# A two-layer trunk on one core: layer 0's adaLN scale in seven blocks of 128 to 512 features in place of five

## The chip, the cores and the metric

The kernel runs on one core of one Trainium2 chip. Its measure is the device time of one execution in microseconds. Three runs of the kernel before gave a median of 1295.17 us, from 1294.84 to 1297.33.

The engines' names in the rows are PE (TensorE, matrix products), PEld (its weight loads), DVE (VectorE), ACT (ScalarE), POOL (GpSimd) and SP (SyncE, which issues most of the loads).

## The reference

A trunk of two layers runs over 128 context tokens and 256 latent tokens, 2048 features each. Before each mixer there is an adaLN step, and layer 0's is where the change lies:

```
m = silu(cond) @ w_mod + b_mod          # (2048 -> 6144), once for c_ctx, once for c
shift, scale, gate = split(m, 3)
h = rms_norm(x, g) * (1 + scale) + shift
proj = h @ w_in                         # q, k, v, conv and gate parts
...
x = x + gate * (concat([a, b]) @ w_out)
```

All is float32. The context tokens take the modulation of c_ctx, the latent tokens that of c. Products of tokens with weights must hold float32 accuracy.

## The kernel before

**Tokens and products.** The state is kept transposed, features on partitions: `xT` is 128 partitions x 16 chunks (k = 0 to 15, 128 features each) x 384 tokens. A product in float32 is made from three matmuls of half-length operands: both operands are split into a high and a low part (`hhi`, `hlo` of the tokens, `whi`, `wlo` of the weights) and hi x hi, hi x lo and lo x hi are added in PSUM. `whi` is a ScalarE cast (L283), `wlo` a VectorE subtraction (L284).

**The scale.** The adaLN vector is a product of two conditioning vectors with a 2048 x 2048 slice of the modulation weights: 16 MiB that are read once, in 16 tiles of 1 MiB. `gemv_block` (L122 to 145) makes one block of `nf` features: one *unit* per tile, with `2048 // nf` matmuls each, that hold a 32-column window of the conditioning vectors `cst` as weights and stream the tile's `nf` columns. Four accumulators stand in the four 32-partition groups of one PSUM tile (`gv`). A finished block is *handed over*: ScalarE copies it (`gs`, L143), PE transposes it in pieces of 128 (L172), VectorE adds the four groups (L158) and the bias (L160), and for the scale forms (1 + s) * g (L163). The PSUM pool of `gv` has one buffer. Tiles land in a ring of four SBUF slots (L592).

**The front of the program.** The loop at L607 to 627 goes over the scale's blocks. For each, with priority, it issues the block's units, the load of the block's part of `xT`, and `make_h`, which forms `hhi` (ScalarE, L289) and `hlo` (VectorE, L290) from `xT` and the scale; then, per chunk k, `q_unit` (L594) loads 512 KB of q weights, splits them and issues 18 matmuls of 512 columns, and `square` gathers the squares for the norm. The norm's own factor (`rs0`, `rb0`) is applied later, so the q products need the scale alone. After it the stage that the text calls wkv makes the k and v products (`tok_unit`, L347, matmuls at L355) on the shifted tokens. Four blocks of 512 features of layer 0's shift are made there in the same manner, one ahead of every four chunks (`shifted`, L643); `hhi` and `hlo` come from L302 and L303.

**What sets the order.** Every engine has one queue of instructions. The order in each is decided by a scheduler that runs the program through a simulated timeline when the kernel is built; a priority (`first()`), a chain that keeps all loads of SP in program order (L95 to 101), and a few added dependences steer it. So where units of a gemv stand between the products is the scheduler's choice, and it can change far behind an edit.

Of the kernel before, what the change touches and what calls it, by code (L numbers as in the profile page):

```python
# [20 lines left out]
D = 2048  # L21
# [22 lines left out]
SCALE_AT = (11,)  # L44
RA = 1.2
RB = 1.1
GRID_W = 64
GROUPS = ((0, 0, SEQ), (1, SEQ, T))

# [2 lines left out]
def trunk(ctx: ExitStack, tc: tile.TileContext, d: dict, o: dict):  # L52
# [25 lines left out]
    def vcol(name, i):  # L78
        return vec(name)[:, i:i + 1]
# [5 lines left out]
    cst = const.tile([P, 2 * KC + 30], F32, name="cst")  # L85
# [61 lines left out]
    def mod_tile(layer, part):  # L147
        m = const.tile([P, KC, 2], F32, name=f"mod{layer}{part}")
        mods[layer, part] = m
        return m  # L150
# [14 lines left out]
    def mod_part(layer, part, widths=(512, 512, 512, 512), f0=0):  # L165
        if (layer, part) not in mods:
            mod_tile(layer, part)

        def consume(f0, nf, gs, pc):
            n = nf // P  # L170
            for i in range(n):
                nc.tensor.transpose(pc[:, i * P:(i + 1) * P], gs[:, i * P:(i + 1) * P], ident)  # L172
            sl = slice(f0 // P, (f0 + nf) // P)
            mod_finish(layer, part, sl, pc[:, :nf].rearrange("p (k g r) -> p k r g", g=4, r=32)[:, :, 0:2, :])
        units = []
        for nf in widths:
            units += gemv_block(d[f"mod_w{layer}"][4 * part + f0 // 512], f0 % 512, nf, lambda k: cst[:, 2 * k:2 * k + 32],
                                lambda gs, ps, f0=f0, nf=nf: consume(f0, nf, gs, ps))
            f0 += nf
        return units  # L180
# [419 lines left out]
                    nc.tensor.matmul(pq[b][t], lhsT=x[:, k, tt], rhs=y[:, 0, 512 * b:512 * b + 512],  # L600
                                     start=(k == 0 and n == 0), stop=(k == KC - 1 and n == 2))

    widths = (256, 256, 512, 512, 512)
    scale_q = mod_part(0, 1, widths)
    pq = [[acc("q0") for t in range(NT)], [acc("q1"), acc("q1"), aux("q1")]]
    av, square = square_sum(nc.gpsimd)
# [151 lines left out]
    def ln_out(c):  # L758
        ln["out"] = nc.vector.tensor_tensor(apad[:, c, :T], apad[:, c, :T], ln["r"], ALU.mult).ins
        nc.scalar.activation(apad[:, c, :T], apad[:, c, :T], AF.Silu, scale=vcol("ln_g0", c), bias=vcol("ln_b0", c))  # L760
    bg["rate"] = RB

# [190 lines left out]
def _by_rows(a):  # L953
    return a.reshape(a.shape[0], -1, P).transpose(2, 1, 0)


def _blocks(w, width):
    return w.reshape(KC, P, -1, width).transpose(2, 1, 0, 3)


def _layout(inputs):
    a = {name: np.asarray(x) for name, x in inputs.items()}
    out = {name: a[name] for name in _AS_IS}
    out["vecs"] = np.concatenate([a[name].reshape(n, P).T for name, n in _VECS], axis=1)
    for name in ("c_ctx", "c"):
        out[f"row_{name}"] = a[name].reshape(-1)
    for l in range(2):
        out[f"modT{l}"] = a[f"mod_w{l}"].T.reshape(48, P, D)
    out["xT"] = _by_rows(np.concatenate([a["x_prompt"][0], a["x_sample"][0]]))
    out["cw"] = _by_rows(np.concatenate([a["conv_w0"], a["short_w1"]]))  # L970
    for l in range(2):
        out[f"cache_k{l}"] = a[f"cache_k{l}"][0].transpose(2, 1, 0)
        out[f"mod_w{l}"] = _blocks(a[f"mod_w{l}"], 512)
        out[f"w_out{l}"] = _blocks(a[f"w_out{l}"], 256)
    w = a["w_in0"]
    out["wf0"] = _blocks(np.concatenate([w[:, :3 * CW], w[:, 3 * CW + 1536:]], axis=1), 256)
    out["wq0"] = _blocks(w[:, 3 * CW:3 * CW + 1024], 1024)
    out["wkv0"] = _blocks(w[:, 3 * CW + 1024:3 * CW + 1536], 512)
    out["wt1"] = _blocks(a["w_in1"][:, :1536], 512)
    out["wf1"] = _blocks(a["w_in1"][:, 1536:], 256)  # L980
    return out


def _tables():
# [3 lines left out]
    tok = np.arange(DEC)  # L988
    ar = (tok // GRID_W).astype(f)[:, None] * inv
    ac = (tok % GRID_W).astype(f)[:, None] * inv  # L990
    ang = np.concatenate([ar, ar, ac, ac], axis=-1).astype(f)
# [26 lines left out]
```

## Time and profile before

| | |
|---|---|
| median of three runs | 1295.17 us (1294.84 to 1297.33) |
| the profiled execution | 1295.11 us |
| its span | 1293.3 us, so 1.81 us lie outside it |
| PE busy | 1260.2 us, 97% of the span |
| VectorE, ScalarE, GpSimd busy | 873.3, 540.3 and 91.7 us |
| DMA | 258.00 MB, mean 199 GB/s |

The span runs from the first to the last recorded instruction of the core. The chain of waits is followed back from the last instruction, at each step to what released it, so its shares say where the end was decided. In a timeline row the first number is the start and the second the length; adjacent matmuls overlap in their recorded lengths, and the distance from start to start is what one costs in a row. A row's `x16` says that it stands for 16 records; a float32 matmul of a gemv unit leaves two, so the 8 matmuls of a 256-wide unit stand as x16 and the 4 of a 512-wide one as x8.

### The profile page before, as it was taken

How to read it: one execution, taken by the hardware profiler on the slowest of the kernel's cores; microseconds unless marked ns; L12 is line 12 of the kernel's file. 1: busy time of each engine (PE TensorE's matmuls, PEld its weight loads, DVE VectorE, ACT ScalarE, POOL GpSimd, SP SyncE). 2: the span in 40 equal slices, each digit the busy share in tenths (PEclk: the TensorE clock that was granted, in tenths of full speed). 3: DMA queues.
4: the chain of work that ended last, by engine and by line, in shares of the span. 5: the costliest groups of instructions: out<-in, count | busy, mean ns of one | idle time of the engine just before them, and what ended most of it. 6: DMA issues, size and time to landing. Idle time of an engine off the chain costs nothing.

```text
span 1293.3 us, 17857 instructions
## 1 busy us (share of the span) xinstructions
PE 1260.2 (97%) x6892; PEld 1114.7 (86%) x6892; DVE 873.3 (68%) x1507; ACT 540.3 (42%) x936; POOL 91.7 (7%) x129
## 2 busy tenths in 40 slices
PE   6999999999999999999999999999999999999996
PEld 4566676778888889999999988899999999999996
DVE  2244688989899867999776933354544599994443
ACT  3345422564455555533363623354444432343331
POOL 0211100000000000111000000000000011101110
PEclk9999999999999999999999999999999999999998
DMA  9989987878665444677543444433333578744322
GB/s 363 402 311 350 346 315 293 324 247 290 225 200 172 169 150 147 187 259 249 163 129 115 131 124 124 138 114 115 99 98 98 171 267 275 261 148 127 119 66 98
DMA packets 70503, 258.00 MB, mean 199 GB/s; under 512 B 7377, under 2 KB 11729, under 8 KB 65425
## 3 DMA queue, kind: packets, MB, share of 16 engines
q1 hardware_dynamic: 58768, 207.71, 47.4%
q0 software_dynamic: 11504, 49.04, 10.8%
q8 instruction: 54, 0.88, 0.3%
q14 instruction: 33, 0.26, 0.1%
q10 hardware_dynamic: 144, 0.10, 0.0%
HBM read 253.15 MB, written 3.67 MB: 199 GB/s over the span
## 4 chain that ended last, share of the span: by engine, by line
PE 95%; issue 2%; DMA 1%; ACT 1%; DVE 1%; POOL 0%; POOLq 0%; SPq 0%; DVEq 0%; ACTq 0%
PE pf L376 67%; PE pt L355 10%; PE q L600 6%; PE gv L139 5%; PE s_ps L499 2%; PE o_ps L524 2%; PE pT_ps L520 1%; DMA ring<-in_mod_w 1%; PE gv L172 1%; PE qT_ps L485 0%; PE gv L664 0%; ACT mix L452 0%; DMA raw<-in_mod_w 0%; DVE y L929 0%; ACT whi L283 0%
## 5 line engine op out<-in xcount | busy, mean ns | idle before, releaser
L376 PE MATMUL pf<-hhi,whi 128*128 128x384 f32 (+1 forms) x1664 | 570.0, 343 | 2.1 <-ACT whi L283 2.1
L376 PE MATMUL pf<-hlo,whi 128*128 128x384 f32 (+1 forms) x1664 | 569.2, 342 | 0.0
L376 PE MATMUL pf<-hhi,wlo 128*128 128x384 f32 (+1 forms) x1664 | 564.5, 343 | 1.2 <-DVE wlo L284 1.2
L284 DVE TENSOR_TENSOR wlo<-raw,whi 128x1024 fp32r<-128x1024 f32 x256 | 312.9, 1223 | 299.3 <-ACT whi L283 294.4
L283 ACT CAST whi<-raw 128x1024 fp32r<-128x1024 f32 x256 | 268.3, 1049 | 485.0 <-PE pf L376 276.5
L376 PEld LDWEIGHTS pf<-hhi,whi 128*128 128x128 f32 x1664 | 313.5, 188 | 24.0 <-issue 14.0
L376 PEld LDWEIGHTS pf<-hhi,wlo 128*128 128x128 f32 x1664 | 313.4, 189 | 15.9 <-issue 7.3
L376 PEld LDWEIGHTS pf<-hlo,whi 128*128 128x128 f32 x1664 | 314.0, 189 | 5.0 <-issue 2.7
L690 DVE SCALAR_TENSOR_TENSOR cv<-apad,cw,cv 128x399 f32<-128x399 f32 x240 | 138.3, 627 | 0.1
L207 DVE CUSTOM_DVE_ANT_0 area<-area,crow 128x1024 f32<-128x1024 f32 x112 | 132.5, 1218 | 4.5 <-PE o_ps L524 4.5
L355 PE MATMUL pt<-wlo,hhi 128*128 128x512 f32 x192 | 75.8, 395 | 0.0
L355 PE MATMUL pt<-whi,hhi 128*128 128x512 f32 x192 | 75.5, 396 | 0.0
L355 PE MATMUL pt<-whi,hlo 128*128 128x512 f32 x192 | 74.2, 396 | 0.0
L91 POOL DMA_DIRECT2D area<-in_modT x56 | 29.6, 529 | 552.0 <-DVE sm L207 206.0
L276 POOL TENSOR_TENSOR sacc<-sacc,sqf 128x384 f32<-128x384 f32 x28 | 33.4, 1194 | 176.3 <-ACT sqf L275 175.5
L600 PE MATMUL q<-whi,hhi 128*128 128x512 f32 x96 | 41.2, 429 | 4.4 <-ACT hhi L289 4.4
L355 PEld LDWEIGHTS pt<-whi,hhi 128*128 128x128 f32 x192 | 36.0, 188 | 10.9 <-ACT hhi L302 1.7
L355 PEld LDWEIGHTS pt<-whi,hlo 128*128 128x128 f32 x192 | 35.9, 188 | 9.9 <-DVE wlo L284 1.7
L355 PEld LDWEIGHTS pt<-wlo,hhi 128*128 128x128 f32 x192 | 36.1, 188 | 9.1 <-issue 0.8
L139 PE MATMUL gv<-ring,cst 128*32 128x512 f32 (+1 forms) x288 | 35.6, 582 | 8.4 <-DMA ring<-in_mod_w 7.5
L507 ACT ACTIVATE pr<-s_ps,nm 128x384 f32<-128x384 f32 (+1 forms) x48 | 24.4, 508 | 45.8 <-DVE nm L506 34.6
L600 PE MATMUL q<-wlo,hhi 128*128 128x512 f32 x96 | 40.6, 423 | 0.0
(181 smaller groups left out, 986.4 us busy)
## 6 DMA issues: line engine op xcount, KB each, us to landing
raw<-in_wf SPq DMA_DIRECT2D x144, 512.0 KB, 4.1
ring<-in_mod_w SPq DMA_DIRECT2D x32, 1024.0 KB, 7.5
raw<-in_w_out SPq DMA_DIRECT2D x64, 512.0 KB, 4.1
area<-in_modT POOLq DMA_DIRECT2D x56, 512.0 KB, 5.3
raw<-in_mod_w SPq DMA_DIRECT2D x48, 512.0 KB, 5.2
raw<-in_wq SPq DMA_DIRECT2D x32, 512.0 KB, 8.9
raw<-in_wt SPq DMA_DIRECT2D x24, 512.0 KB, 3.5
lent<-in_modT POOLq DMA_DIRECT2D x8, 1024.0 KB, 8.2
```

The costliest lines, as they stand in the source:

```text
L91: ins = nc.gpsimd.dma_start(dst, src).ins
L139: nc.tensor.matmul(ps[32 * g:32 * g + 32, :nf], lhsT=stat(k), rhs=raw[:, i % raw.shape[1], :], start=(k < 4), stop=(k >= KC - 4))
L207: ins = nc.vector.tensor_tensor_reduce(out=raw if g else junk, in0=raw, in1=crow[:, g, h * n:(h + 1) * n], scale=1.0, scalar=0.0, op0=ALU. ...
L276: eng.tensor_tensor(av, av, s, ALU.add)
L283: nc.scalar.copy(dst_hi, src)
L284: order["split"] = nc.vector.tensor_tensor(dst_lo, src, dst_hi.bitcast(F32), ALU.subtract).ins
L355: nc.tensor.matmul(pp[t], lhsT=x[:, k, tt], rhs=y[:, i, :], start=(k == 0 and n == 0), stop=(k == KC - 1 and n == 2))
L376: ins = nc.tensor.matmul(pp[j][:, :n], lhsT=x[:, i, fj], rhs=y[:, k, :n], start=(begin and k % 8 == 0 and m == 0), stop=(end and k % 8 == ...
L499: nc.tensor.matmul(ps, lhsT=mix[:, h0 + h, t * P:(t + 1) * P], rhs=kT[:, kv, c0:c0 + nk * P], start=True, stop=True)
L524: nc.tensor.matmul(po, lhsT=v[:, slots[j], kv * HD:(kv + 1) * HD], rhs=pT[:, j, :], start=(j == 0), stop=(j == nk - 1))
L600: nc.tensor.matmul(pq[b][t], lhsT=x[:, k, tt], rhs=y[:, 0, 512 * b:512 * b + 512], start=(k == 0 and n == 0), stop=(k == KC - 1 and n == 2))
L690: nc.vector.scalar_tensor_tensor(st["o"], apad[:, c, j:j + CVW], cw[:, c, j:j + 1], st["o"], ALU.mult, ALU.add)
```

## The change

The list `widths` has seven blocks in place of five. For blocks under 512 wide the weights come from new arrays, `scale128` (features 0 to 255) and `scale256` (features 256 to 1023), which hold the same numbers laid out block by block: per block 128 partitions, then 16 chunks, then the block's features in a row. A tile for the ring is then one piece of 8 KB per partition; before, a 256-wide block was cut from a 512-wide one, in eight pieces of 1 KB per partition. The blocks of 512 are read as before. The same bytes are read, and 128-wide blocks have one unit of 16 matmuls of 128 columns each. Lines after the insertions stand 1 (from L44) to 5 (from L179 on) further down in the changed kernel: L139 is L140 there, L172 is L173, L158 is L159, L160 is L161, L284 is L289, L303 is L308, L355 is L360, L600 is L605.

```
--- before.py
+++ after.py
@@ -44,6 +44,7 @@
 SCALE_AT = (11,)
 RA = 1.2
 RB = 1.1
+NARROW = {128: (0, 256), 256: (256, 1024)}
 GRID_W = 64
 GROUPS = ((0, 0, SEQ), (1, SEQ, T))
 
@@ -174,7 +175,11 @@
             mod_finish(layer, part, sl, pc[:, :nf].rearrange("p (k g r) -> p k r g", g=4, r=32)[:, :, 0:2, :])
         units = []
         for nf in widths:
-            units += gemv_block(d[f"mod_w{layer}"][4 * part + f0 // 512], f0 % 512, nf, lambda k: cst[:, 2 * k:2 * k + 32],
+            if nf < 512:
+                w, at = d[f"scale{nf}"][(f0 - NARROW[nf][0]) // nf], 0
+            else:
+                w, at = d[f"mod_w{layer}"][4 * part + f0 // 512], f0 % 512
+            units += gemv_block(w, at, nf, lambda k: cst[:, 2 * k:2 * k + 32],
                                 lambda gs, ps, f0=f0, nf=nf: consume(f0, nf, gs, ps))
             f0 += nf
         return units
@@ -600,7 +605,7 @@
                     nc.tensor.matmul(pq[b][t], lhsT=x[:, k, tt], rhs=y[:, 0, 512 * b:512 * b + 512],
                                      start=(k == 0 and n == 0), stop=(k == KC - 1 and n == 2))
 
-    widths = (256, 256, 512, 512, 512)
+    widths = (128, 128, 256, 256, 256, 512, 512)
     scale_q = mod_part(0, 1, widths)
     pq = [[acc("q0") for t in range(NT)], [acc("q1"), acc("q1"), aux("q1")]]
     av, square = square_sum(nc.gpsimd)
@@ -972,6 +977,8 @@
         out[f"cache_k{l}"] = a[f"cache_k{l}"][0].transpose(2, 1, 0)
         out[f"mod_w{l}"] = _blocks(a[f"mod_w{l}"], 512)
         out[f"w_out{l}"] = _blocks(a[f"w_out{l}"], 256)
+    for nf, (f0, f1) in NARROW.items():
+        out[f"scale{nf}"] = _blocks(a["mod_w0"][:, D + f0:D + f1], nf)
     w = a["w_in0"]
     out["wf0"] = _blocks(np.concatenate([w[:, :3 * CW], w[:, 3 * CW + 1536:]], axis=1), 256)
     out["wq0"] = _blocks(w[:, 3 * CW:3 * CW + 1024], 1024)
```

The scheduler's order differs on all engines at many small places in the first third of the program. PE's queue at the start of the kernel before (`gv` is a block's accumulator, `ring` the loaded tiles, `q0` and `q1` the q accumulators):

```order
L139 MATMUL gv_108<-ring_98,cst_87 32x256 x16
L172 MATMUL gv_108<-ident_79,gs_127 128x128 x2
L600 MATMUL q0_101<-whi_145,hhi_93 128x512
L600 MATMUL q0_101<-wlo_146,hhi_93 128x512
L600 MATMUL q0_102<-whi_145,hhi_93 128x512
```

and of the changed kernel:

```order
L140 MATMUL gv_108<-ring_98,cst_87 32x128 x16
L173 MATMUL gv_108<-ident_79,gs_126 128x128
L140 MATMUL gv_162<-ring_98,cst_87 32x128 x16
L605 MATMUL q0_101<-whi_139,hhi_93 128x512
L605 MATMUL q0_101<-wlo_140,hhi_93 128x512
```

The order groups like rows: before, the first `x16` holds the units of both tiles, 8 matmuls each. Now the first block is a single tile of 16 narrower matmuls and one transpose, and the second block's unit stands ahead of the first q product.

PE's queue in the wkv stage of the kernel before, where the second block of the shift is handed over (`pt0` to `pt2` are the k and v accumulators of the three token groups):

```order
L355 MATMUL pt2_790<-whi_979,hlo_94 128x512
L139 MATMUL gv_1001<-ring2_99,cst_87 32x512 x4
L139 MATMUL gv_1001<-ring_98,cst_87 32x512 x4
L172 MATMUL gv_1001<-ident_79,gs_1022 128x128 x4
L139 MATMUL gv_1106<-ring_98,cst_87 32x512 x4
L355 MATMUL pt0_788<-whi_1060,hhi_93 128x512
```

and of the changed kernel:

```order
L360 MATMUL pt2_836<-whi_1025,hlo_94 128x512
L140 MATMUL gv_1047<-ring2_99,cst_87 32x512 x4
L140 MATMUL gv_1047<-ring_98,cst_87 32x512 x4
L173 MATMUL gv_1047<-ident_79,gs_1068 128x128 x4
L360 MATMUL pt0_834<-whi_1106,hhi_93 128x512
L360 MATMUL pt0_834<-wlo_1107,hhi_93 128x512
```

The first unit of the next shift block (`gv_1106`) stood between the transposes and the first product; now the product follows the transposes, and that unit (`gv_1152`) comes nine products later.

VectorE's queue at the same handover, before:

```order
L284 TENSOR_TENSOR wlo_1061<-raw_1058,whi_1060 128x1024
L284 TENSOR_TENSOR wlo_1085<-raw_1082,whi_1084 128x1024
L158 TENSOR_REDUCE mod00_787<-gv_1001 128x8
L160 TENSOR_TENSOR mod00_787<-mod00_787,vecs_81 128x8
L303 SCALAR_TENSOR_TENSOR hlo_94<-h32_1030,mod00_787,hhi_93 128x128
```

and of the changed kernel:

```order
L159 TENSOR_REDUCE mod00_833<-gv_1047 128x8
L161 TENSOR_TENSOR mod00_833<-mod00_833,vecs_81 128x8
L289 TENSOR_TENSOR wlo_1107<-raw_1104,whi_1106 128x1024
L289 TENSOR_TENSOR wlo_1131<-raw_1128,whi_1130 128x1024
L308 SCALAR_TENSOR_TENSOR hlo_94<-h32_1076,mod00_833,hhi_93 128x128
```

The two weight splits stood ahead of the reduction of the finished block and stand behind it now. Further on, around 211 us of the profile before, VectorE's queue had one of its 128x2048 modulation sums (`lent`) ahead of the split `wlo_1651`:

```order
L717 TENSOR_TENSOR apad_1235<-pf1_1421,sgb_1418 128x256
L207 ISA lent_1239,sm101_1254<-lent_1239,crow_91 128x2048
L207 ISA sm101_1254 128x1
L284 TENSOR_TENSOR wlo_1651<-raw_1648,whi_1650 128x1024
L284 TENSOR_TENSOR wlo_1681<-raw_1678,whi_1680 128x1024
```

and the changed kernel has:

```order
L722 TENSOR_TENSOR apad_1281<-pf0_1466,sgb_1462 128x256
L289 TENSOR_TENSOR wlo_1697<-raw_1694,whi_1696 128x1024
L722 TENSOR_TENSOR apad_1281<-pf1_1467,sgb_1464 128x128
L722 TENSOR_TENSOR apad_1281<-pf1_1467,sgb_1464 128x256
L289 TENSOR_TENSOR wlo_1727<-raw_1724,whi_1726 128x1024
L212 ISA lent_1285,sm101_1300<-lent_1285,crow_91 128x2048
```

Both splits now stand ahead of that sum, the first of them between the products' evacuations (`apad`).

## Rows read from the trace of the kernel before

**Rows 1.** The page: span, busy time by engine (share, instructions), chain by line.
```profile
span 1293.3 us, 17857 instructions
...
PE 1260.2 (97%) x6892; PEld 1114.7 (86%) x6892; DVE 873.3 (68%) x1507; ACT 540.3 (42%) x936; POOL 91.7 (7%) x129
...
PE pf L376 67%; PE pt L355 10%; PE q L600 6%; PE gv L139 5%; PE s_ps L499 2%; PE o_ps L524 2%; PE pT_ps L520 1%; DMA ring<-in_mod_w 1%; PE gv L172 1%; PE qT_ps L485 0%; PE gv L664 0%; ACT mix L452 0%; DMA raw<-in_mod_w 0%; DVE y L929 0%; ACT whi L283 0%
```

**Rows 2.** Chain of waits, first 30 us; columns start us, length us, what.
```profile
1.66 7.70 DMA ring<-in_mod_w
...
21.31 1.00 PE gv L139 x16
22.31 0.43 PE q L600
22.74 0.55 PE gv L139 x4
...
23.72 0.99 PE gv L139 x12
24.71 3.90 PE q L600 x16
28.61 0.23 PE gv L172 x2
```

**Rows 3.** Timeline of the start; idle before and its releaser in brackets.
```profile
6.52 1.94 PE L139 MATMUL gv<-ring,cst 128*32 128x256 f32 x16 [6.52 <-DMA ring<-in_mod_w]
6.92 0.22 PEld L139 LDWEIGHTS gv<-ring,cst 128*32 128x32 f32 x4 [0.20 <-issue]
...
9.40 1.93 PE L139 MATMUL gv<-ring,cst 128*32 128x256 f32 x16 [0.95 <-DMA ring<-in_mod_w]
...
12.96 1.04 ACT L283 CAST whi<-raw 128x1024 fp32r<-128x1024 f32 x1 [0.23 <-DMA raw<-in_wq]
...
14.71 0.80 PE L600 MATMUL q<-whi,hhi 128*128 128x512 f32 x1 [2.19 <-ACT hhi L289]
...
18.29 0.63 PE L600 MATMUL q<-whi,hhi 128*128 128x512 f32 x1
...
18.71 0.63 PE L600 MATMUL q<-wlo,hhi 128*128 128x512 f32 x1
...
21.24 1.07 PE L139 MATMUL gv<-ring,cst 128*32 128x256 f32 x16
...
29.10 1.07 PE L139 MATMUL gv<-ring,cst 128*32 128x512 f32 x8 [0.27 <-DVE mod L158]
```

**Rows 4.** Windows; busy us and (x instructions), PE clock, DMA share, GB/s.
```profile
14.70:19.50 4.80, 4.79 (x11) 3.84 (x12) 1.97 (x5) 1.05 (x3) 0.00 (x0) 1.00 1.09 364
...
42.00:54.00 12.00, 9.04 (x40) 6.16 (x36) 5.55 (x14) 6.64 (x13) 0.00 (x0) 0.86 1.01 415
140.00:155.00 15.00, 13.76 (x77) 7.76 (x72) 8.26 (x20) 5.57 (x12) 1.95 (x3) 1.00 0.98 381
```

**Rows 5.** Timeline of PE, first product after the long handover.
```profile
45.72 0.50 PE L600 MATMUL q<-whi,hhi 128*128 128x512 f32 x1 [2.20 <-ACT hhi L289]
```

**Rows 6.** Timeline of two handovers in the wkv stage.
```profile
127.76 1.07 PE L139 MATMUL gv<-ring,cst 128*32 128x512 f32 x8 [0.28 <-DVE mod L158]
127.94 2.19 ACT L302 ACTIVATE hhi<-h,mod 128x128 fp32r<-128x128 f32 x6 [2.00 <-DVE mod L160]
...
128.76 0.51 PE L355 MATMUL pt<-whi,hhi 128*128 128x512 f32 x1
...
142.20 1.07 PE L139 MATMUL gv<-ring,cst 128*32 128x512 f32 x8 [0.35 <-DVE mod L158]
```

**Rows 7.** Timeline around 211 to 215 us, VectorE and the product behind it.
```profile
211.41 2.28 DVE L207 CUSTOM_DVE_ANT_0 lent<-lent,crow 128x2048 f32<-128x2048 f32 x1
...
213.61 2.35 DVE L284 TENSOR_TENSOR wlo<-raw,whi 128x1024 fp32r<-128x1024 f32 x2
...
214.89 0.44 PE L376 MATMUL pf<-hhi,wlo 128*128 128x384 f32 x1 [1.19 <-DVE wlo L284]
```

More of the change, by code (lines that the diff above doesn't have):

```diff
@@ L46 @@
 RB = 1.1
+NARROW = {128: (0, 256), 256: (256, 1024)}
 GRID_W = 64
@@ L176, in mod_part @@
         for nf in widths:
-            units += gemv_block(d[f"mod_w{layer}"][4 * part + f0 // 512], f0 % 512, nf, lambda k: cst[:, 2 * k:2 * k + 32],
+            if nf < 512:
+                w, at = d[f"scale{nf}"][(f0 - NARROW[nf][0]) // nf], 0
+            else:
+                w, at = d[f"mod_w{layer}"][4 * part + f0 // 512], f0 % 512
+            units += gemv_block(w, at, nf, lambda k: cst[:, 2 * k:2 * k + 32],
                                 lambda gs, ps, f0=f0, nf=nf: consume(f0, nf, gs, ps))
@@ L601, in q_unit @@
                                      start=(k == 0 and n == 0), stop=(k == KC - 1 and n == 2))
-    widths = (256, 256, 512, 512, 512)
+    widths = (128, 128, 256, 256, 256, 512, 512)
     scale_q = mod_part(0, 1, widths)
@@ L974, in _layout @@
         out[f"w_out{l}"] = _blocks(a[f"w_out{l}"], 256)
+    for nf, (f0, f1) in NARROW.items():
+        out[f"scale{nf}"] = _blocks(a["mod_w0"][:, D + f0:D + f1], nf)
     w = a["w_in0"]
```

## The prediction, made before the changed kernel was timed

> **What bounds the kernel now.** I read the page's busy shares first, then the chain of waits, then the windows and the timeline of the places that the change touches. TensorE (PE) is busy 1260.2 of 1293.3 us and holds most of the chain that ended last; DMA has 1% of it [rows 1]. So a microsecond counts only where PE stands idle, runs at the lower clock, or gets more to do. PE idles 33 us in all, and the front of the kernel has a good part of it. The chain of the first 30 us is DMA until 9.36, then come the second 1 MiB scale tile's matmuls, transposes, a VectorE/ScalarE handover, and the first q product at 14.71, which waited 2.19 us behind the transposes [rows 2, 3]. So the first scale block, not the q weights, sets when the products start. The weight loads do not set it: k=1's raw tile had landed by 12.96 [rows 3]. Later the chain is almost all PE, with a handover (copy, transposes, reduce, add, hhi) wherever a finished block gates the next products.
>
> The clock shows as spacing. At 18.29 and 18.71 two q products start 0.42 us apart, and a chain piece at 24.71 has 16 in 3.90 [rows 2, 3], 0.24 each: the levels 1.2 and 2.4 GHz. The window 14.70 to 19.50 prints 1.00 in its clock column although the products in it are 0.42 apart, so there I go by spacing; 42 to 54 prints 0.86, and it is the window of PE's 2.20 us wait before 45.72 [rows 4, 5]: (1 - 0.86) x 12 = 1.7 us lost at the lower level.
>
> **The change part by part.** The bytes stay the same: 16 tiles of 1 MiB for the scale. What changes is the blocks' size (128, 128, 256, 256, 256, 512, 512 features), the DMA pieces (8 KB in a row per partition, where 256-wide blocks took eight of 1 KB), and with these the scheduler's order up to about a third of the kernel.
>
> *Start.* Before, two tiles must land and two units of 8 matmuls run before the first block is whole. Now one tile gives block 0, features 0 to 127, enough for k=0. The loads now stand as tile, xT, raw, tile, xT, raw. How fast do they land? The first tile's unit starts at 6.52, the second's at 9.40 [rows 3], each as its tile lands: 1024 KB in 2.88 us, 356 KB/us. From 9.40 to the cast of k=1's raw tile at 12.96 come 384 KB of xT and two raw tiles, 1408 KB in 3.56 us, 395 KB/us. At 395 each tile saves 2.88 - 1024/395 = 0.29 us. Tile 1 then lands near 6.2. Its unit, transpose, reduce, add and hhi for k=0 need less than the five microseconds to 11.4, and k=0's raw tile lands near 8, so none of these is late. What is late is PE itself: in its new order the second block's unit stands ahead of the first q product. Its tile has 704 KB more before it than before (one xT part of 192 and one raw of 512): 704/395 = 1.78, so 9.40 + 1.78 - 2 x 0.29 = 10.60, say 10.65. Bounds: 10.2, if the overlap of transfers hides some of the 704, and 11.2, if short pieces never cost anything. A 128-wide unit is 16 matmuls of 128 columns, and no row shows one. The profile has two records for each float32 matmul, so a 256-wide unit (8 of 256 columns) stands as x16, 1.94 at the lower clock, and a narrow one would stand as x32. If each record cost what it does at 256 columns, it would be 3.9, the upper bound. The lower is 1.07, a unit at the higher clock. At that clock 16 records of 256 columns (21.24) and 8 of 512 (29.10) both take 1.07 [rows 3], so the columns set it, and they are the same in a narrow unit: I take 1.94. First q product: 10.65 + 1.94 + about 0.1 = 12.7 in place of 14.71, **-2.0 us**. From above +0.5 (tile at 11.2 and unit of 3.9: 15.2). From below -2.9 with the unit at the higher clock. Since PE now goes from the unit straight into the products, without the pause of 2.19, its clock may also rise sooner: five products at 0.24 in place of 0.42 would be 0.9 more, -3.8 in all. I count none of it, since no row shows when the clock rises after such a start.
>
> *Skill against row.* The window 42 to 54 moves 415 GB/s for 12 us [rows 4]. "DMA: Bandwidth & Descriptors" of the Trainium skill, section Specifications, gives about 358 GB/s as the HBM limit of one core. By that limit the 356 KB/us of the first two tiles would already be the ceiling, contiguous pieces would win nothing, the second tile would land at 11.2 and the sum would be 0.55 higher. The trace disagrees, since 415 is held.
>
> *Skill against row.* Weight loads at 6.92 lie inside the matmul stretch that runs from 6.52 to 8.46 [rows 3]. "TensorE: Matmul & The Clock Gate" of the Trainium skill, section The mechanism, says loads overlap matmuls in flight only where the row groups differ. Here all 128 rows are always in use, so by that rule a narrow unit, with twice the loads, would go toward 3.9 and the first product toward 14.7. The trace disagrees with the strict form.
>
> *Handovers in the q stage.* Two more 256-wide handovers come before the long ones. One costs, beside the unit itself, the transposes' 0.23 and the 0.27 that PE waits for the reduce [rows 2, 3]: 0.45 to 0.64 with the switches, so +1.1 for two. The transposes of one four-transpose handover go (4 x 0.115, -0.45), and a unit that ran in two cut pieces now runs whole: before, 0.43 and 0.55, 0.43 once more, and 0.99 [rows 2] for two products and the unit's 16 records, which in one piece are 2 x 0.24 + 1.00 = 1.48; -0.9, of which I take -0.8 for the switch that stays. Net **-0.1**. The long wait (2.20 before 45.72, and the 1.7 us lost at the lower level) does not vanish: the same sort of handover now stands before k=8, at about 60 us. Its cover is the same, so 0. DMA is not late there: a 512-wide block brings 6.75 MiB (scale 4, raw 2, xT 0.75), 17.1 us at the 415 GB/s of [rows 4], and PE needs 72 x 0.24 and 4 x 1.0, 21.3.
>
> *The wkv stage.* Here the new order is worse for PE. Before, right after the transposes PE ran the next block's first unit from 127.76, while ScalarE made hhi from 127.94; products went on at 128.76 [rows 6]. Now the products stand right behind the transposes, and the unit comes nine products later. The products can start near 127.94 + 0.36 + 0.05 = 128.35, 0.41 sooner, but the unit is paid later by itself: 1.2 (its 1.07, and 0.51 where a product in a row shows about 0.4 [rows 6]). So +0.8 each at two handovers, this one and the next (142.20, [rows 6]): +1.6. The unit comes in more pieces (+0.5). On VectorE the reduce and add now stand ahead of both wlo subtractions, 1.2 each as the pair of 2.35 [rows 7], which before were done by then; so the second product waits for wlo, +0.5, and hlo behind it, +0.3, and the copy gs +0.1. Sum **+3.0**; bounds +0.5 (the scheduler's view, all hidden but one unit's share) and +5 (both handovers also uncover the second wlo).
>
> *VectorE at 211.* PE waits 1.19 us at 214.89 for wlo, which stood behind a 2.28 us reduction on VectorE [rows 7]. In the new order that wlo stands ahead of the reduction, between the apad products. The idle goes: **-1.2**, bounds 0 (the raw tile or the cast is next) and -1.5.
>
> Everything else: VectorE +6 and ScalarE +4 small instructions, hidden beside PE; the order moves in many small places to about 560 us, with no sign that I can read: 0, bounds +-1.5.
>
> **Sum.** -2.0 - 0.1 + 3.0 - 1.2 = -0.3. The profiled execution took 1295.11 us, 1293.3 of them span. 1295.11 - 0.3 = **1294.8 us**; the median of the runs shown is 1295.17, 0.06 above the profiled one.
>
> **Rivals.** What a measurement of this kernel tells from no change is 0.2%, 2.6 us.
>
> 1. Faster: the long handover before k=8 comes while PE has products in hand, so its clock does not fall (-1.7), and the wkv handovers cost 1.2 in place of 3.0 (-1.8): 1291.3. For it: in the old order the block of features 1024 to 1535, the same one, was handed over before k=8 with products in hand. Against: the same unhidden chain of copy, transposes, reduce and hhi stands there in the new order.
> 2. Slower: the uncovered wkv handovers (no unit between transposes and products) bring the clock down, as after the wait at 45.72. Price 1.7 each, twice: 1294.8 + 3.4 = 1298.2. It decides from the point where PE's idle there resembles that of 42 to 45.7; before, the window 140 to 155 held 1.00 with shorter waits [rows 4], so it needs about a microsecond or more of extra idle.
> 3. The change doesn't do what it says: tile 2 at 11.2 and a unit at 3.9 us put the first product at 15.2, or shorter pieces bring nothing. Then the start gives +0.5 in place of -2.0: 1297.3, still within 0.2%.
>
> **How the numbers follow.** Forecast 0.40, rival 3 0.12, rival 1 0.28, rival 2 0.20. The forecast and rival 3 lie within 0.2% of 1295.17 (1292.6 to 1297.8); rival 1 is faster, and rival 2 slower: faster 0.28, same 0.52, slower 0.20. Range 1291.0 to 1298.8: from a little under rival 1 to a little over rival 2; the forecast alone, by its own terms' bounds, has 1292.5 to 1297.5.
>
> **What would show it.** The first q product at 12.7 and the second gv unit from 10.65 for 1.94; its neighbours' spacing falling to 0.24 sooner than at 19. In the wkv stage gv units standing behind products, idle of 0.8 or so before the first product of each block, and a wait for wlo. At 211, no wait of 1.2 for wlo. The prediction is wrong in its middle if the wkv windows differ from before by under 1 us or over 5, or if a clock dip appears or goes.

## The result, and the profile after

The changed kernel took **1303.74 us** (median of 6 runs, 1300.11 to 1307.91), the kernel before 1295.26 beside it (6 runs). The ratio is 1.0061, 95% interval 1.004 to 1.0083: slower by about 8.5 us, and outside the range of the prediction, which had 1294.8 and a range of 1291.0 to 1298.8. Its runs spread over 7.8 us, those of the kernel before over 2.5. The profiled execution is the slowest of the six, 1307.91 us, so its differences are shown by stage and then weighed with runs of other kernels.

The page of the changed kernel, against [rows 1]: PE is busy 8.3 us longer in a span 12.8 us longer, and VectorE and DMA hold 2% each of the chain, where they had 1% each.

```profile
span 1306.1 us, 17993 instructions
...
PE 1268.5 (97%) x6956; PEld 1121.8 (86%) x6956; DVE 875.0 (67%) x1513; ACT 543.4 (42%) x940; POOL 91.0 (7%) x129
...
PE 93%; DVE 2%; DMA 2%; ACT 1%; issue 1%; SPq 0%; DVEq 0%; ACTq 0%
```

The same line of the kernel before:

```profile
PE 95%; issue 2%; DMA 1%; ACT 1%; DVE 1%; POOL 0%; POOLq 0%; SPq 0%; DVEq 0%; ACTq 0%
```

The start, against [rows 3] (timeline; idle before and its releaser in brackets). The first product comes at 13.53 in place of 14.71, and the products are 0.24 apart from 17.53 on (three in 0.87; in the kernel before from 19.52 on). The copy `gs` of the first block stood behind a cast on ScalarE that waited for a raw tile (9.05), PE's transpose waited 2.00 us for it, and the handover ended at 11.62 (L161). The second unit starts at 11.66. Its tile came at the same moment: the load was issued at 2.60 and landed 8.9 us later, at 11.52, and the unit starts 0.14 behind that, as the first one starts 0.13 behind its tile (6.24 and 6.37). So either alone would have put the unit there, and the late copy by itself cost next to nothing.

```profile
6.37 1.94 PE L140 MATMUL gv<-ring,cst 128*32 128x128 f32 x32 [6.37 <-DMA ring<-in_scale]
...
9.05 1.04 ACT L288 CAST whi<-raw 128x1024 fp32r<-128x1024 f32 x1 [1.04 <-DMA raw<-in_wq]
10.00 0.26 ACT L144 COPY gs<-gv 128x128 f32<-128x128 f32 x1
...
10.31 0.48 PE L173 MATMUL gv<-ident,gs 128*128 128x128 f32 x1 [2.00 <-ACT gs L144]
...
11.46 0.16 DVE L161 TENSOR_TENSOR mod<-mod,vecs 128x2 f32<-128x2 f32 x1
...
11.66 1.94 PE L140 MATMUL gv<-ring,cst 128*32 128x128 f32 x32 [0.87 <-DVE mod L161]
...
13.53 0.80 PE L605 MATMUL q<-whi,hhi 128*128 128x512 f32 x1
...
17.53 0.87 PE L605 MATMUL q<-whi,hlo 128*128 128x512 f32 x3
18.24 0.39 PE L605 MATMUL q<-whi,hhi 128*128 128x512 f32 x1
18.47 0.39 PE L605 MATMUL q<-wlo,hhi 128*128 128x512 f32 x1
...
66.76 0.79 PE L605 MATMUL q<-whi,hhi 128*128 128x512 f32 x1 [2.62 <-ACT hhi L294]
```

The last of these rows ends the long wait of the q stage, now before k=8. The load of the second tile, in the list of loads issued between 2.5 and 2.7 us (KB, us to landing):

```profile
ring<-in_scale SPq DMA_DIRECT2D x1, 1024.0 KB, 8.9
```

The wkv stage, against [rows 6]. No unit stands between the transposes and the first product; PE waits 0.99 us for `hhi` at one handover and 1.54 at the next, and `wlo` and `hlo` come behind the reduce. No product waits for that `wlo`: the second one follows the first by 0.34 us (129.23), as in the kernel before (128.76 and 129.10).

```profile
128.32 1.22 DVE L289 TENSOR_TENSOR wlo<-raw,whi 128x1024 fp32r<-128x1024 f32 x1
128.44 2.19 ACT L307 ACTIVATE hhi<-h,mod 128x128 fp32r<-128x128 f32 x6 [0.30 <-DVE mod L161]
128.89 0.50 PE L360 MATMUL pt<-whi,hhi 128*128 128x512 f32 x1 [0.99 <-ACT hhi L307]
129.23 0.39 PE L360 MATMUL pt<-wlo,hhi 128*128 128x512 f32 x1
...
129.46 1.40 DVE L308 SCALAR_TENSOR_TENSOR hlo<-h,mod,hhi 128x128 fp32r<-128x128 f32 x4
...
144.77 0.50 PE L360 MATMUL pt<-whi,hhi 128*128 128x512 f32 x1 [1.54 <-ACT hhi L307]
```

Behind it, against [rows 7]. A gemv unit for the q bias waits 2.08 us for its raw tile, which the kernel before did not. A product waits 1.60 us for a `wlo` behind another 2.29 us sum on VectorE than in [rows 7]; the wait of 1.19 that [rows 7] has is gone. At 250.49 there is a wait of 3.10. The kernel before has two in that place, 1.36 and 1.45, so little was added there (and new_blocks_old_order below has 2.96).

```profile
193.88 1.05 PE L140 MATMUL gv<-raw,mix 128*32 128x512 f32 x4 [2.08 <-DMA raw<-in_wq]
...
206.05 1.12 PE L669 MATMUL gv<-gs,mix 128*128 128x512 f32 x2 [0.69 <-ACT gs L144]
...
207.81 2.29 DVE L212 CUSTOM_DVE_ANT_0 lent<-lent,crow 128x2048 f32<-128x2048 f32 x1
...
210.10 1.22 DVE L289 TENSOR_TENSOR wlo<-raw,whi 128x1024 fp32r<-128x1024 f32 x1
...
211.37 0.44 PE L381 MATMUL pf<-hhi,wlo 128*128 128x384 f32 x1 [1.60 <-DVE wlo L289]
...
250.49 0.69 PE L381 MATMUL pf<-hhi,whi 128*128 128x384 f32 x1 [3.10 <-ACT whi L288]
```

The two of the kernel before:

```profile
238.65 1.05 PE L139 MATMUL gv<-raw,cst 128*32 128x512 f32 x4 [1.36 <-DMA raw<-in_mod_w]
...
241.16 0.57 PE L376 MATMUL pf<-hhi,whi 128*128 128x384 f32 x1 [1.45 <-ACT whi L283]
```

The chain of waits tells how the raw tile came to be late. Its load was issued at 182.04, behind three other loads that SP issued from 180.15 on, and took 11.79 us. In the kernel before the same tile's load was issued at 178.58, took 6.8 us and had landed 7 us ahead of its unit (192.50). The chain of the changed kernel, then the load in the kernel before:

```profile
182.04 11.79 DMA raw<-in_wq
193.83 0.04 issue
193.88 1.05 PE gv L140 x4
```

```profile
raw<-in_wq SPq DMA_DIRECT2D x1, 512.0 KB, 6.8
```

Windows of the changed kernel (PE clock is the third last column), to [rows 4]. The clock column is below 1.00 in four of them: (1 - 0.83) x 20 = 3.4 us lost, 1.8, 3.4 and 1.8. It stays at 1.00 in 140 to 155, behind the waits of the wkv stage. The kernel before lost 1.7 in 42 to 54 and 1.8 in 240 to 260. Below, a *clock stretch* is a piece of the clock record at 1.2 GHz that costs 1.7 us, half of its length; a piece of twice the length counts as two.

```profile
60.00:80.00 20.00, 16.62 (x71) 10.44 (x72) 6.57 (x14) 8.07 (x16) 3.54 (x3) 0.83 0.87 345
140.00:155.00 15.00, 12.70 (x69) 7.10 (x69) 9.69 (x22) 7.35 (x13) 1.06 (x2) 1.00 0.99 368
180.00:200.00 20.00, 17.92 (x93) 14.54 (x93) 14.68 (x15) 4.23 (x5) 1.60 (x3) 0.91 0.96 359
240.00:260.00 20.00, 16.90 (x77) 11.93 (x76) 19.60 (x38) 13.24 (x50) 0.00 (x0) 0.83 0.97 370
280.00:300.00 20.00, 18.02 (x99) 12.08 (x98) 18.47 (x31) 11.85 (x27) 1.61 (x3) 0.91 0.69 224
```

and of the kernel before:

```profile
240.00:260.00 20.00, 18.84 (x93) 15.66 (x94) 19.29 (x38) 7.66 (x16) 0.00 (x0) 0.91 0.76 263
```

**PE's loss by stage.** Both kernels give PE the same work in another order. So I counted for every matmul record about the spacing that it has in a row at 2.4 GHz (0.2305 us for 512 columns of a product and 0.1745 for 384, where the trace's medians are 0.232 and 0.175, and 1.0 for a gemv unit of 1 MiB; the small error is the same in every kernel), and took the sum of what had been started from the time. The growth of that difference is what PE lost, whatever the order. Of it I took half of the time at 1.2 GHz as the clock's part, at the start by the products' spacing, behind it by the clock record. The stages are cut at the same amounts of work (10, 88, 156, 192, 600 us); "start" counts from the first tile's landing.

| us lost, net of the clock / by the clock | start | q | wkv | to 192 | 192 to 600 |
|---|---|---|---|---|---|
| kernel before | 3.05 / 6.46 | 6.98 / 1.71 | 6.73 / 0 | 7.80 / 0 | 32.59 / 1.71 |
| changed kernel | 1.89 / 5.57 | 7.44 / 3.41 | 10.17 / 0 | 11.96 / 1.71 | 33.31 / 5.12 |
| new_blocks_old_order | 2.06 / 4.52 | 8.24 / 1.71 | 6.70 / 0 | 7.83 / 0 | 32.55 / 1.71 |
| old_blocks_new_order | 3.04 / 6.57 | 6.99 / 1.71 | 10.15 / 0 | 12.10 / 3.41 | 32.86 / 0 |
| new_order_in_wkv_only | 1.55 / 4.62 | 8.28 / 1.71 | 9.81 / 0 | 7.83 / 0 | 32.67 / 0 |
| new_order_behind_wkv_only | 1.35 / 4.94 | 7.38 / 3.41 | 5.76 / 0 | 11.45 / 0 | 31.91 / 3.41 |
| old_wkv_in_new_places | 1.75 / 4.66 | 8.24 / 1.71 | 7.01 / 0 | 11.73 / 1.71 | 31.90 / 5.12 |
| blocks_of_256_early_norm | 1.56 / 4.75 | 4.43 / 0 | 9.69 / 0 | 7.80 / 0 | 33.29 / 1.71 |

The net losses repeat to a few tenths where the order is the same; the clock's part does not. In the q stage the two trade: where there are two clock stretches, the first begins while PE still waits (at 65.32 in the changed kernel, whose product starts at 66.76), and the net loss is some 0.8 lower.

### The profile page after: what moved, and what is told of

It reads as the page before. It is cut to its first block, busy times and chain, and to the rows that moved or that the text cites. A ratio compares the mean times of both kernels' runs of the same rounds, so it can differ in the third digit from the quotient of the medians.

```text
span 1306.1 us, 17993 instructions
## 1 busy us (share of the span) xinstructions
PE 1268.5 (97%) x6956; PEld 1121.8 (86%) x6956; DVE 875.0 (67%) x1513; ACT 543.4 (42%) x940; POOL 91.0 (7%) x129
## 4 chain that ended last, share of the span: by engine, by line
PE 93%; DVE 2%; DMA 2%; ACT 1%; issue 1%; SPq 0%; DVEq 0%; ACTq 0%
PE pf L381 65%; PE pt L360 10%; PE q L605 6%; PE gv L140 5%; PE s_ps L504 2%; PE o_ps L529 2%; DMA raw<-in_wq 1%; PE pT_ps L525 1%; DVE cv L695 1%; DMA raw<-in_wf 1%; ACT whi L288 1%; PE y_ps L907 1%; DVE wlo L289 0%; PE qT_ps L490 0%; PE gv L173 0%
## 5 line engine op out<-in xcount | busy, mean ns | idle before, releaser
L289 DVE TENSOR_TENSOR wlo<-raw,whi 128x1024 fp32r<-128x1024 f32 x256 | 313.9, 1227 | 288.7 <-ACT whi L288 283.8
L360 PE MATMUL pt<-whi,hhi 128*128 128x512 f32 x192 | 75.6, 397 | 2.5 <-ACT hhi L307 2.5
L360 PE MATMUL pt<-wlo,hhi 128*128 128x512 f32 x192 | 75.7, 394 | 0.0
L360 PE MATMUL pt<-whi,hlo 128*128 128x512 f32 x192 | 75.2, 398 | 0.0
L360 PEld LDWEIGHTS pt<-whi,hhi 128*128 128x128 f32 x192 | 36.0, 188 | 13.8 <-ACT hhi L307 3.8
L360 PEld LDWEIGHTS pt<-whi,hlo 128*128 128x128 f32 x192 | 35.9, 188 | 12.8 <-DVE hlo L308 2.0
L605 PE MATMUL q<-whi,hhi 128*128 128x512 f32 x96 | 41.4, 431 | 2.6 <-ACT hhi L294 2.6
L140 PE MATMUL gv<-ring,cst 128*32 128x512 f32 (+2 forms) x352 | 35.3, 510 | 8.4 <-DMA ring<-in_scale 6.4
L360 PEld LDWEIGHTS pt<-wlo,hhi 128*128 128x128 f32 x192 | 36.1, 188 | 8.1
L605 PE MATMUL q<-wlo,hhi 128*128 128x512 f32 x96 | 40.6, 422 | 0.0
```

What stands on the lines that cost most here:

```text
L140: nc.tensor.matmul(ps[32 * g:32 * g + 32, :nf], lhsT=stat(k), rhs=raw[:, i % raw.shape[1], :], start=(k < 4), stop=(k >= KC - 4))
L289: order["split"] = nc.vector.tensor_tensor(dst_lo, src, dst_hi.bitcast(F32), ALU.subtract).ins
L360: nc.tensor.matmul(pp[t], lhsT=x[:, k, tt], rhs=y[:, i, :], start=(k == 0 and n == 0), stop=(k == KC - 1 and n == 2))
```

## The experiments

**Holding the order.** Behind the loop over the blocks both kernels issue the same instructions. So I wrote each engine's final order of one kernel into a table and chained the other's instructions by it; nothing waits longer for that, only who stands ahead of whom on an engine is fixed (abridged: the unpacking of the table is left out):

```
+    ins = nc.cur_bb.bb.instructions[start:]      # start: behind the loop, or a stage's border
+    for row in table:                            # one row for each engine
+        for p, q in zip(row, row[1:]):
+            tc.add_manual_dep(ins[q], ins[p].name, NOSYNC, reason="order kept")
```

All runs below were timed beside the kernel before, which had medians of 1295.4 to 1295.5. No run holds a kernel in its own order with nothing else changed. Two come near: old_blocks_new_layout and changed_weights_before_sum lie about 1 us under the kernels whose order they hold, so nothing suggests that the table itself costs much.

*new_blocks_old_order*: the changed kernel, table of the kernel before, from the loop's end on.

> The changed kernel, with the instructions that come behind the q products in the program held in the order, engine by engine, in which the kernel before has them. The front (seven blocks, new arrays) stays as changed. Theory A (the loss is the scheduler's new order behind the q stage, the blocks themselves gain about what the first pt product shows, 116.38 against 117.21): 1294.4 us, 0.8 under the kernel before. Rival B (the loss follows the new front, by way of the clock or the loads, whatever the order behind it): 1303 to 1304.

Measured: 1292.59 us (10 runs; ratio to the kernel before 0.9977, 95% interval 0.9968 to 0.9986; the brackets below read the same). **The change of the blocks is a gain of 2.8 us** when nothing else moves, more than the 0.8 of theory A.

*old_blocks_new_order*: the kernel before, table of the changed one.

> The kernel before (five blocks, old arrays), with the instructions behind the q products held in the changed kernel's order. Theory A: the loss without the gain, 1295.3 + 9.3 = 1304.5 us. Rival B: 1295.3, as before. If both have a part, between: the distance from 1295.3 over 9.3 is the share of the order.

Measured: 1305.10 us (5 runs; 1.0074, 1.0062 to 1.0086). **The new order costs 9.7 us** without any new block. With the new blocks it costs 1303.7 - 1292.6 = 11.2, and 11.2 lost and 2.8 gained make the 8.5. Rival B falls. The wait for the raw tile is longer here, and two clock stretches begin with it:

```profile
194.69 1.92 PE L201 MATMUL gv<-raw,mix 128*32 128x512 f32 x4 [2.75 <-DMA raw<-in_wq]
```

*new_order_in_wkv_only* and *new_order_behind_wkv_only*: the changed kernel with the old table for one of the two stages, its own for the other.

> The changed kernel with its own order in the wkv stage, and the old order behind it. Theory A1 (order; the wkv stage loses the 4.0 us that the profiles show between the first pt and the first pf product, the rest behind it): 1295.3 - 0.8 + 4.0 = 1298.4. Theory A2 (order; the wkv stage is all of it, and what is later follows from being late there): 1303 to 1304. Rival B: 1303 to 1304 as well.

> The changed kernel with the old order in the wkv stage and its own order behind it. Theory A1: 1295.3 - 0.8 + 5.3 = 1299.7 (5.3 is the rest of the 8.5 between the medians, so clock windows included). Theory A2: 1294.5. Rival B: 1303 to 1304. In the trace, A1 has the waits at 193.88, 206, 211.37 and 250.49 again, with 2.08, 0.69, 1.60 and 3.10 us, and pt products that follow a gemv unit as in the kernel before.

Measured: 1294.65 us (11 runs; 0.9997, 0.9988 to 1.0006) and 1294.33 (12 runs; 0.9992, 0.9984 to 1.0001). Theory A2 falls. A1 has the places right, but 2.1 and 1.7 us over 1292.59 do not make the 11.2 of the changed kernel. In the second, the scheduler had mixed the border of the stages anew: four `pf` products stand ahead of the last handover's transposes, and products run while ScalarE makes `hhi`; its wkv loss is 5.76 where the old order has 6.7.

```profile
154.91 0.44 PE L446 MATMUL pf<-hhi,whi 128*128 128x384 f32 x1
...
155.74 0.66 PE L238 MATMUL gv<-ident,gs 128*128 128x128 f32 x4
156.15 0.42 PE L446 MATMUL pf<-hhi,wlo 128*128 128x384 f32 x1
```

*old_wkv_in_new_places*: the changed kernel's table with the wkv instructions in the old order in the wkv places, so that the border stays.

> The changed kernel in its own order behind the q products, but with the wkv stage's instructions in the old order among themselves, put into the places that the wkv stage has in the new order (new_order_behind_wkv_only let the scheduler mix the two stages anew, and there four pf products hid the last handover). Theory A4 (the order behind the wkv stage costs about 2.7 us net of the clock, and the 1.7 us of new_order_behind_wkv_only are less because the newly mixed border gives 1.3 back): 1292.6 + 2.7 + up to 1.7 for a clock window at the wait for the raw tile = 1295.3 to 1297.0. Rival A5 (the two stages' orders cost more only together): 1294.3, as new_order_behind_wkv_only. Rival A6 (the border itself is what costs): over 1299.

Measured: 1300.19 us (10 runs; 1.0029, 1.0019 to 1.0039), above A4's range: A6's number, but not for its reason alone. With the border held the order behind the wkv stage costs 1300.2 - 1292.6 = 7.6, and the wkv stage's own order on top of it 1303.7 - 1300.2 = 3.5 (alone it cost 2.1). Net of the clock the profile has 0.3 + 3.9 for the two stages, 1.5 more than new_order_behind_wkv_only has, of which the border is 1.25. Most of the rest is clock: over all its runs (1 - granted clock) x span is 9.3 us, 9.6 in the changed kernel, 6.3 in new_blocks_old_order and 7.2 in new_order_behind_wkv_only. So 4.2 net and 3.0 of clock make 7.2 of the 7.6, and for the changed kernel 3.5 + 4.1 net and 3.3 of clock make 10.9 of its 11.2. The same sum gives 3.6 for new_order_behind_wkv_only, which lost 1.7, so it is good to about 2 us, and why that run is 5.9 us faster than this one is in part open. The raw tile is waited for again, and the sum again:

```profile
188.52 1.05 PE L202 MATMUL gv<-raw,mix 128*32 128x512 f32 x4 [1.86 <-DMA raw<-in_wq]
...
206.01 0.45 PE L443 MATMUL pf<-hhi,wlo 128*128 128x384 f32 x1 [1.60 <-DVE wlo L351]
```

*changed_pf_before_handover*: the changed kernel's own table, on PE 4 `pf` moved ahead of the last transposes and 16 ahead of the next 6 `pt`.

> The changed kernel, every engine in its own order behind the q products, with one exception on PE: at the last handover of the shift the first 4 pf products stand ahead of the transposes and 16 more ahead of the next 6 pt products (in new_order_behind_wkv_only the scheduler had put them so). Theory A3 (the new order in the wkv stage and the one behind it cost more together than alone, 8.4 us more than new_blocks_old_order's 1292.6 by 2.1 and 1.7, in part because this handover is uncovered: 1.68 us there against 0.06): 1.5 us faster than the changed kernel, 1302.2. If the handover is also what makes the later wait for the raw tile long enough for a clock window: 1299 to 1300. Rival: what is uncovered here is paid later by the same pf products, 1303.7.

Measured: 1305.20 us (6 runs; 1.0073, 1.0056 to 1.009). A miss: no gain, and the interval overlaps that of the changed kernel. ScalarE and VectorE kept their order, so the `pf` products now wait for their own weights. What comes of moving those engines' instructions as well was not tried.

```profile
160.02 0.44 PE L443 MATMUL pf<-hhi,whi 128*128 128x384 f32 x1 [1.65 <-ACT whi L350]
...
163.12 0.44 PE L443 MATMUL pf<-hhi,wlo 128*128 128x384 f32 x1 [1.69 <-DVE wlo L351]
```

*changed_weights_before_sum*: the changed kernel's own table, one `wlo` moved ahead of one sum.

> The changed kernel in its own order, with one VectorE instruction moved: the weight split wlo whose product waits 1.60 us at 211.37 stands ahead of the 2.29 us sum (207.81) in place of behind it. The term that the prediction had as -1.2 and that came out as a wait at another sum: if the sum is what it waits for, 1.0 to 1.5 us faster than the changed kernel's 1303.7 (the cast whi, which ends near 207.9, then sets it, and the evacuations nat behind it): 1302.4. Rival: the wait passes to nat or to the next product, 1303.7.

Measured: 1302.69 us (5 runs; 1.0054, 1.0042 to 1.0066). The median is 1.05 us lower, near what was expected, but the two intervals overlap, so the gain is not shown. In the trace the wait of 1.60 is gone, and later waits have grown: one of 0.49 at 233.16, and 3.86 at 247.69 where the changed kernel has 3.10.

```profile
206.13 1.22 DVE L351 TENSOR_TENSOR wlo<-raw,whi 128x1024 fp32r<-128x1024 f32 x1
...
207.27 2.28 DVE L274 CUSTOM_DVE_ANT_0 lent<-lent,crow 128x2048 f32<-128x2048 f32 x1
```

**Layout and blocks, with the old order behind the loop.**

*new_blocks_read_in_place*: `w, at = d[f"mod_w{layer}"][4 * part + f0 // 512], f0 % 512` for all blocks, the front's order held too.

> The seven blocks, read from the 512-wide layout of before (pieces of 512 bytes for the 128-wide blocks and 1 KB for the 256-wide, no new arrays), the front held in the changed kernel's order and what is behind it in the old order: it differs from new_blocks_old_order (1292.59 us) in the layout alone. Theory L1 (the smaller first block is what gains, and short pieces cost the 0.3 us a tile that 356 against 395 KB/us gives, on the first two tiles): 1293.2, first q product 0.6 us later. Rival L2 (the layout is what gains): 1295.4 or more. Rival L3 (512-byte pieces are dearer than the 1 KB rows show): 1294 to 1295, with the second tile's unit more than 1 us late.

*old_blocks_new_layout*: `widths = (256, 256, 512, 512, 512)`, `NARROW = {256: (0, 512)}`, every engine's order that of the kernel before.

> The five old blocks, the two of 256 read from an array in which each block is one piece of 8 KB per partition; every engine's order is that of the kernel before. It differs from the kernel before in the layout alone. L1: 0.6 us faster, 1294.8. L2: 1292.6. If pieces of 1 KB cost nothing: 1295.4.

Measured: 1295.60 us (11 runs; 0.9998, 0.9989 to 1.0007) and 1294.43 (11 runs; 0.9994, 0.9985 to 1.0003). For the old blocks the layout gives 0.9 us, near the 0.6 of L1, though its interval holds 1. For the new ones it is worth 3.0, so L1 was too small by far; the time is L2's, and without the layout the seven blocks gain nothing. But L2 would have had 1292.6 for the layout alone. So neither part gains clear of noise by itself, and the 2.8 needs both. L3's place was wrong: the second unit is not later against the first (5.44 and 5.47 us). A later tile is, which no longer keeps up with PE:

```profile
28.93 1.07 PE L209 MATMUL gv<-ring,cst 128*32 128x256 f32 x16 [1.03 <-DMA ring<-in_mod_w]
```

With the new layout the same unit waits 0.27 for the reduce:

```profile
26.95 1.07 PE L201 MATMUL gv<-ring,cst 128*32 128x256 f32 x16 [0.27 <-DVE mod L220]
```

From landing to 88 us of work the profiles differ by 1.5 us, the first tile lands 0.45 later, and a clock stretch at 277.88, which the other profile does not have, is worth 1.7. How much of the last two is the layout's stays open.

*one_block_of_256*: `widths = (128, 128, 256, 512, 512, 512)`.

> Blocks of 128, 128, 256, 512, 512, 512; what is behind the q products in the old order. The long handover stands before k=4 as in the kernel before, and two narrow handovers are gone. Theory C1: the start's gain and the old long wait: 1292.6 - 2 x 0.6 = 1291.4 if the clock window behind the long wait is one of 3.4 us, as in the kernel before. Rival C2: no gain from fewer handovers, 1292.6. If the gain of new_blocks_old_order came from moving the long wait to k=8 rather than from the start: 1295.

Measured: 1292.41 us (10 runs; 0.9981, 0.997 to 0.9992). Not to be told from new_blocks_old_order, as C2 had it. The gain is not from where the long wait stands.

*blocks_of_256_throughout*: `widths = (128, 128) + (256,) * 7`, `NARROW = {128: (0, 256), 256: (256, 2048)}`.

> Blocks of 128, 128 and seven times 256, all from contiguous arrays; what is behind the q products in the old order. Theory C1 (the four-transpose handover before k=8 is what costs the q stage: 0.76 and 2.61 us of waits and at least one 3.4 us window at the lower clock, 1.7; a 256-wide handover costs 0.34 of wait and 0.23 of transposes): against new_blocks_old_order -5.1 for the long one, +4 x 0.6 for the narrow ones that come in its place: 1292.6 - 2.7 = 1289.9, with one clock window fewer in the front. Rival C2 (narrow blocks only move the wait to hhi or to the ring's loads): 1292.6 or more, with waits of 1 us or more in the q stage.

Measured: 1293.79 us (11 runs; 0.9984, 0.9975 to 0.9993). C1 missed by 3.9 us, and C2's time came for another reason. The q stage's loss falls as C1 says (one 2.6 us wait is gone), but the norm's row comes later, since the last block is shorter; eight VectorE steps that need it stand ahead of the shift's reduce, and PE waits 2.99 us with a clock stretch from 110.19 on:

```profile
107.51 2.72 DVE L361 SCALAR_TENSOR_TENSOR h<-xT,mod,rb 128x128 f32<-128x128 f32 x8 [0.82 <-ACT rb L328]
110.15 0.18 DVE L220 TENSOR_REDUCE mod<-gv 128x8 f32<-128x32 f32 x1
...
110.39 1.08 PE L201 MATMUL gv<-ring,cst 128*32 128x512 f32 x4 [2.99 <-DVE mod L220]
```

*blocks_of_256_early_norm*:

```
-            sync_load(x["T"][:, k0:k0 + n, :], d["xT"][:, k0:k0 + n, :])
+            m = 4 if k0 == 12 else n
+            if k0 < 14:
+                sync_load(x["T"][:, k0:k0 + m, :], d["xT"][:, k0:k0 + m, :])
...
-        last = j == len(widths) - 1
-        if last:
+        last = k0 >= 12
+        if k0 == 12:
...
-            elif k == k0 + 1:
+            elif k == 13:
```

> blocks_of_256_throughout, with the last four chunks of xT loaded together and squared early, so that the norm's row rb0 is made some 20 products sooner; what is behind the q products in the old order. Theory C1 (the q stage without the long handover gains, and what ate it was one wait of 2.99 us and a clock window at 110.39, where the reduce stood behind eight scale_norm steps that waited for rb0): 1293.8 - 3.0 - 1.6 = 1289.2. Rival C2: the wait is taken over by the next step (wlo, hhi), 1292 or more.

*early_norm_pf_before_handover*: the same, with `pf` moved on PE as above.

> blocks_of_256_early_norm, and at the last handover of the shift 4 pf products ahead of the transposes and 15 more ahead of the next 6 pt products. The wait of 0.76 us there and the slow start behind it go: 1.3 us faster than blocks_of_256_early_norm, 1287.9 if that is 1289.2. Rival: PE's wait only moves to the pt products, no difference.

Measured: **1290.81 us** (5 runs; 0.9967, 0.9955 to 0.9979) and 1293.65 (11 runs; 0.9983, 0.9975 to 0.9992). The first is 4.6 us faster than the kernel before; against new_blocks_old_order the intervals overlap. A wait of 2.05 us at the reduce is left, so C1's 1289.2 is not reached. The q stage runs at the full clock and nearly without idle:

```profile
108.98 1.92 PE L201 MATMUL gv<-ring,cst 128*32 128x512 f32 x16 [2.05 <-DVE mod L220]
```

```profile
40.00:60.00 20.00, 19.66 (x129) 13.70 (x132) 9.58 (x18) 8.85 (x18) 3.58 (x4) 1.00 1.02 412
60.00:80.00 20.00, 19.73 (x131) 14.24 (x124) 8.33 (x14) 8.19 (x15) 7.06 (x6) 1.00 0.90 350
```

In new_blocks_old_order the second of these windows reads:

```profile
60.00:80.00 20.00, 16.63 (x75) 10.37 (x74) 6.56 (x14) 8.65 (x17) 4.38 (x4) 0.91 0.92 363
```

The second is a miss for the same reason as changed_pf_before_handover: its `pf` products wait 1.71 us for `whi` at 151.72 and 1.70 for `wlo` at 154.82.

## Why the prediction was wrong, step by step

*Start, -2.0.* The size came out: by 10 us of work the changed kernel had lost 1.89 + 5.57 = 7.46 us where the kernel before had 9.51, so -2.05. That is in part luck, since two errors cancel. The first product came at 13.53 and not 12.7, because the second tile landed at 11.52 and not near 10.65, and the first block's handover ended no sooner; in the other profiles that begin with the same two tiles it landed at 10.70 to 12.58, each time 0.13 to 0.14 ahead of its unit. And PE reached 2.4 GHz 2.0 us sooner (17.53 against 19.52), which is worth 0.9 (6.46 - 5.57); the prediction had named that and counted it at nothing. "None of these is late" was wrong of the copy, which cost next to nothing beside the tile. The narrow unit took 1.94 with its 32 records, as worked out from the columns.

*Handovers of the q stage, -0.1.* Too good. Net of the clock they are +0.5 in this profile and +1.3 in new_blocks_old_order (8.24 - 6.98), where the clock's loss is the same as before. The long wait went to k=8 as said, but it is 2.62 there (66.76) and not the 2.20 that was taken over, and what else makes the 1.3 was not taken apart. In this profile the clock lost 3.4 us behind the long wait where the price was 1.7; five of the eight profiles with that wait had 1.7.

*wkv, +3.0.* Right in size and in its main part: 10.17 - 6.73 = +3.4, with products that wait for `hhi` and units paid later. The parts differ: the waits are longer than the 0.8 that was told (0.99 and 1.54), and the +0.5 at each handover for a product that waits for `wlo` does not appear, though `wlo` stands behind the reduce as said. By the runs the order of this stage costs 2.1 alone and 3.5 on top of the rest.

*VectorE at 211, -1.2.* Wrong in sign. The sum and the `wlo` that the prediction looked at had changed places, and their wait is gone, but in the same new order another `wlo` came to stand behind another sum, and PE waited 1.60. Looking at one place of an order says nothing on the sum over its places.

**The step that failed** is "the order moves in many small places to about 560 us, with no sign that I can read: 0, bounds +-1.5". It put the rest of the order at nothing without a reason. Between 156 and 192 us of work that order lost 4.2 us net of the clock (11.96 - 7.80): waits of 2.08 at the raw tile, 1.60 at the sum and 0.69 at the copy, where the kernel before had the 1.19 of [rows 7]; the last 1.0 no row here tells apart. Behind these waits come clock stretches. In all the order behind the wkv stage is worth +7.6 by the runs with the border held, and 1.7 where the scheduler mixed the border anew. That place had a row in the prediction for a single term, and its bounds were set by nothing.

*The range.* The prediction gives 1292.5 to 1297.5 as the forecast by its own terms' bounds. Added up, those bounds give 1289.6 to 1302.0, so the stated range of 1291.0 to 1298.8 was narrower than the working behind it; even 1302.0 is under what was measured.

*Rivals.* Rival 2 named the clock, but at the wkv handovers; there the clock column of 140 to 155 stays at 1.00 behind waits of 0.99 and 1.54. The extra clock stretches came behind the longer waits at 66.76, 193.88 and 250.49, and one behind a wait of 1.98 at 287.29. Rival 3 and the faster rival did not happen.

## What to carry to other kernels

Where a scheduler sets the order, an edit has two effects, its own and the order's, and here the second (+9.7 to +11.2 us) was some four times the first (-2.8) and of the other sign; hold the order to measure the first, and then choose the order. Look first at where the new order asks for a tile or a result: here the longest new wait behind the wkv stage came from a load that was issued 10 us before PE was ready for its unit in place of 14, and took 12 us in place of 7. Forecast the order's part from all the places where it changed what PE waits for, and give it the width of what such places cost in the profile, not a width around zero. When blocks at the start are made smaller, look also at what stands at the end of their loop: here the norm's row, which a shorter last block delays.

## What the runs showed of the hardware

Waits in the same place brought different clock losses. Behind the wait for the raw tile the record has no clock stretch with 1.42 us (new_order_behind_wkv_only), one with 1.86 (old_wkv_in_new_places), 2.08 (the changed kernel) and 2.27 (changed_weights_before_sum), none with 2.46 (changed_pf_before_handover), and two with 2.75 (old_blocks_new_order). The long wait of 2.62 us before k=8 had one behind it in five profiles and two in three. So the length of a wait does not tell its price alone. The changed kernel's runs, with more such waits, have mean granted clocks from 0.989 to 0.996, and spread over 7.8 us. In the kernels that begin with the same 128-wide tile the first unit started at 6.30 to 7.69 us, so a microsecond at the start of one profile is not a finding.

How a tile is cut into pieces shows in its landing. In the same order, the second 1 MiB tile landed 2.97 us behind the first in pieces of 1 KB per partition (the kernel before, 6.39 and 9.36; 2.98 in old_blocks_new_order) and 2.50 us behind it in pieces of 8 KB (old_blocks_new_layout, 6.25 and 8.75). And twice as many weight loads cost a gemv unit nothing: at 1.2 GHz 16 matmuls of 128 columns took 1.94 us, as 8 of 256 did.
